# Down projections of a two-layer trunk: 24 instead of 18 of 44 weight pairs by seven products, 16 of them with weight block sums made in DRAM

## The chip, the cores and the metric

The kernel runs on one core of a Trainium2 chip. The metric is the device time in microseconds of one execution. Before the change it is 2559.3 us, the median of 3 runs (2558.61 to 2559.44).

## What is computed

One sequence of 256 tokens with a width of 2048 goes through two layers in float32: a retention layer and a block-sparse attention layer, each followed by a gated MLP with a causal convolution of three taps. D_FF is 5632. The part that is changed is the last product of each MLP:

```python
def conv_ffn(h, w_up, conv_w, conv_b, w_down):
    u = h @ w_up
    ch = u.shape[-1]
    u = lax.conv_general_dilated(
        u, conv_w.astype(u.dtype)[:, None, :], window_strides=(1,),
        padding=[(CONV_WIDTH - 1, 0)], dimension_numbers=('NWC', 'WIO', 'NWC'),
        feature_group_count=ch) + conv_b
    gate, val = jnp.split(u, 2, axis=-1)
    return (jax.nn.silu(gate) * val) @ w_down
...
    for i in range(DEPTH):
        ...
        h = h + conv_ffn(rms_norm(h, ffn_norm[i]), ffn_w_up[i], ffn_conv_w[i], ffn_conv_b[i], ffn_w_down[i])
    return rms_norm(h, final_norm)
```

`w_down` is 5632 x 2048 in each layer.

## The kernel before

**Precision.** Each float32 operand is split into a high part in fp32r and the remainder, and a product is three matmuls: high x high, high x low, low x high. The activations are split once and stay in SBUF (`actT`, `hT`, `yT`, `oT`). The weights stream in from DRAM, and each piece is split on the way: ACT writes `wh` (L226), DVE writes `wl` = `raw` - `wh` (L227), both in `split_to`.

**Units and halves.** A *unit* is 1 MB of weights, loaded by SP into one of four `raw` buffers (`issue_dma`, L168). It is split and used in *halves*: `step` issues the splits up to three halves ahead of the matmuls of the current half (`LOOKAHEAD`), and there are four buffers for `wh` and four for `wl`, one for each half in turn. A load waits until the unit four places back has been split. `later` holds functions that are run when a given half has been reached (`after`).

**Stages.** Eight retention heads, the retention's out projection, the up stage of layer 0 (44 panels of 4 halves, `panel_b`), its down projection, the attention, its out projection, the up stage of layer 1 and its down projection. A down projection is two panels (`panel_s`), one for each 1024 columns of `w_down`; a panel runs over 22 *pairs* of k blocks (2 x 128 rows).

**Eight and seven.** A pair is a product of 2 x 2 blocks: two k blocks of 128 rows, two blocks of 128 tokens, two blocks of 512 columns. Done plainly (`eight`) it is eight block products, 24 matmuls, in two halves of 12. Done by Strassen's method in Winograd's form (`seven`) it is seven, 21 matmuls, in four halves of 6, 3, 6 and 6. A seven needs sums of weight blocks and sums of activation blocks. DVE makes the weight sums in place in the `raw` buffer: L242 after the first half's split, L247 and L248 after the second's; the third and the fourth half's splits read them. The activation sums (*forms*) are made by DVE in the up stage, stored to DRAM (L1021), fetched by ACT's queue into one of eight slots in `hT` (L440) and split there by ACT and DVE (L445, L446) one pair before they are used.

**Order.** A string of letters gives each panel's order, A for a plain pair and S for a seven. Before, the first panel of a down projection has ten sevens, at the odd places from 3 to 21, and the second has eight, "AAASASASASASASASASAAAA". So in both panels each seven stands behind a plain pair. The order on each engine is then set by a scheduler that may move an instruction by a few places.

Of the kernel before, what the change touches and what calls it, by code (L numbers as in the profile page):

```python
# [17 lines left out]
P = 128  # L18
# [50 lines left out]
def wide_seqs(first, second, n_slots=8):  # L69


    n = len(second)
    one = [(p, first.index(p) % n_slots if p in first else None, p in first) for p in range(n)]
    again = [(i % n_slots, p, False) for i, p in enumerate(first)][-n_slots:]
    again += [(again[i][0], p, True) for i, p in enumerate(first[:-n_slots])]
    again = again[: second.count("S")]
    others = [p for p in range(n) if p not in [q for _, q, _ in again]]
    two = []
    for c in second:
        slot, p, fresh = again.pop(0) if c == "S" else (None, others.pop(0), False)  # L80
        two.append((p, slot, fresh))
    return one, two


def head_seq(pairs, seq, fresh):

    again, others = list(enumerate(pairs)), [p for p in range(len(seq)) if p not in pairs]
    return [(*again.pop(0)[::-1], fresh) if c == "S" else (others.pop(0), None, False) for c in seq]


FFN_SEVENS = list(range(3, 22, 2))
FFN_SEQS = wide_seqs(FFN_SEVENS, "AAASASASASASASASASAAAA")
RET_SEQS = wide_seqs([5, 7, 9, 11, 13, 15], "AAASASASASASAAAA")
HEAD_SEQS = [head_seq([0, 2, 4], "AASASASA", hd == 0) for hd in range(RH - 1)] + [head_seq([0, 2], "AASAASAA", False)]
MOB_V_SEQ = head_seq([0, 2, 4], "AASASASA", True)
MOB_SEQS = wide_seqs([3, 5, 7], "AAASAAAA")


def build(tc, a, out):
# [44 lines left out]
    halves = []  # L144
    state = {"dma": 0, "split": 0, "mm": 0}
# [93 lines left out]
    def split_b11_b22(raw, wh, wl):  # L239
        b = blocks(raw)  # L240
        split_to(blocks(wh), blocks(wl), b[:, 0:4:3, :])
        dve.tensor_tensor(b[:, 0:2, :], b[:, 0:4:3, :], b[:, 1:2, :].to_broadcast([P, 2, 512]), op=ALU.add)  # L242

# [121 lines left out]
    def panel_s(unit, xT, seq, temps, done, slots=hT_slot, end=None, before=None,  # L365
                stored=None):
# [42 lines left out]
        def fs(s, i):  # L409
            return [v[:, i * P : (i + 1) * P] for v in slots(s)]  # L410
# [39 lines left out]
        def seven(i, k, s):  # L450
# [151 lines left out]
    def out_proj(w, seqs, xT, temps, g0, use_r, stored=None):  # L602
# [9 lines left out]
        emit(panel_s(unit_s(w, 0), xT, seqs[0], temps, residual_s(0, temps), stored=stored))  # L612
        emit(panel_s(unit_s(w, 1024), xT, seqs[1], temps,
                     residual_s(2, temps, lambda: [transpose_first(i) for i in range(2)], rest), stored=stored))
# [242 lines left out]

    xT_h = [hT]
# [42 lines left out]
    for hd in range(RH):  # L901
        ret_head(hd)
# [86 lines left out]
    def ffn_layer(layer, begin, g_next, use_next, last):  # L989
# [5 lines left out]

        for j in range(NFB // 2):
# [28 lines left out]
        if not last:  # L1025
            return out_proj(wd, FFN_SEQS, actT, temps_ffn, g_next, use_next, stored)
# [7 lines left out]
        emit(panel_s(unit_s(wd, 0), actT, FFN_SEQS[0], temps_ffn, residual_s(0, temps_ffn), stored=stored))  # L1034
        emit(panel_s(unit_s(wd, 1024), actT, FFN_SEQS[1], temps_ffn, residual_s(2, temps_ffn, last=last_bank), end=4,
                     before=gains_first, stored=stored))
# [208 lines left out]
```

## Time and profile before

| | |
|---|---|
| median of 3 runs | 2559.3 us |
| the profiled execution | 2559.53 us |
| its span | 2557.4 us |
| DVE busy | 2107.6 us, 2766 instructions |
| ACT busy | 1447.6 us, 1870 instructions |
| POOL busy | 10.2 us, 24 instructions |
| moved by DMA | 504.41 MB, 197 GB/s on average |

The span runs from the first to the last instruction of the program. PE is TensorE's matmuls, PEld its weight loads (which run beside the matmuls), DVE VectorE, ACT ScalarE, POOL GpSimd, SP SyncE, which issues most loads. In lines of instructions, "L227 DVE TENSOR_TENSOR wl<-raw,wh" is an instruction of line 227 on DVE that writes the tile wl from raw and wh; "x3" merges three of them that follow one another; "[0.41 <-ACT wh L226]" says that the engine had been idle for 0.41 us and what ended that. Matmuls are pipelined: each takes longer than the distance to the next, so their starts are what to compare.

### The profile page before, as it was taken

The numbers are of one execution on the slowest core, as the hardware profiler recorded it, in microseconds if no ns is written. First come the engines' busy times: TensorE is split into PE (matmuls) and PEld (weight loads), VectorE is DVE, ScalarE is ACT, GpSimd is POOL, SyncE is SP. The second block draws the span as 40 slices with busy tenths as digits, with TensorE's granted clock in tenths as the row PEclk, the third lists the DMA queues.
The fourth block names the chain that finished last, engine by engine and source line by source line (L and its number), as shares of the span: only waits on it lengthen the run. The fifth ranks groups of instructions, "written<-read, shape, count | busy, mean of one in ns | idle before, by whom it ended". The sixth has DMA issues, their size and how long they took to land.

```text
span 2557.4 us, 34487 instructions
## 1 busy us (share of the span) xinstructions
PE 2545.5 (100%) x13277; PEld 2177.8 (85%) x13277; DVE 2107.6 (82%) x2766; ACT 1447.6 (57%) x1870; POOL 10.2 (0%) x24
## 2 busy tenths in 40 slices
PE   9999999999999999999999999999999999999998
PEld 8888888888888888888888888888888888888887
DVE  7888888998877777777898887768877777778997
ACT  6555555555565555555565655555655555555654
POOL 0000000000000000000000000000000000000000
PEclk9999999999999999999999999999999999999999
DMA  7665655555565656566665565555565656567654
GB/s 258 227 201 186 197 186 186 189 181 196 199 197 183 205 188 203 190 202 193 235 208 193 198 216 179 174 183 172 193 196 194 198 191 200 193 199 243 214 198 148
DMA packets 342196, 504.41 MB, mean 197 GB/s; under 512 B 9600, under 2 KB 260496, under 8 KB 341776
## 3 DMA queue, kind: packets, MB, share of 16 engines
q1 hardware_dynamic: 330672, 483.53, 57.2%
q10 hardware_dynamic: 11360, 18.69, 2.2%
q8 instruction: 104, 1.70, 0.3%
q14 instruction: 60, 0.49, 0.1%
HBM read 494.82 MB, written 10.51 MB: 198 GB/s over the span
## 4 chain that ended last, share of the span: by engine, by line
PE 95%; DVE 3%; ACT 1%; issue 1%; DMA 1%; SPq 0%; POOL 0%; POOLq 0%; ACTq 0%; DVEq 0%
PE acc L349 34%; PE aux L395 31%; PE acc L352 17%; PE acc L395 8%; DVE wl L227 1%; PE acc L315 1%; PE acc L317 1%; PE acc L316 1%; PE aux L529 0%; PE aux L528 0%; PE aux L527 0%; PE aux L545 0%; DMA raw<-in_ret_w_in_dram 0%; ACT wh L226 0%; PE acc L545 0%
## 5 line engine op out<-in xcount | busy, mean ns | idle before, releaser
L226 ACT ACTIVATE wh<-raw 128x1024 fp32r<-128x1024 f32 (+2 forms) x1067 | 1084.2, 1027 | 1005.4 <-PE acc L349 434.6
L227 DVE TENSOR_TENSOR wl<-raw,wh 128x1024 fp32r<-128x1024 f32 (+2 forms) x1067 | 1242.8, 1182 | 388.9 <-ACT wh L226 381.1
L349 PE MATMUL acc<-hT,wh 128*128 128x512 f32 x3840 | 1197.7, 393 | 1.0 <-DVE hT L551 0.8
L352 PEld LDWEIGHTS acc<-hT,wl 128*128 128x128 f32 x3840 | 720.4, 188 | 161.4 <-DVE wl L227 0.6
L352 PE MATMUL acc<-hT,wl 128*128 128x256 f32 x3840 | 761.3, 279 | 0.2 <-DVE wl L227 0.2
L349 PEld LDWEIGHTS acc<-hT,wh 128*128 128x128 f32 x3840 | 586.3, 188 | 3.0 <-ACT wh L226 1.6
L395 PE MATMUL aux<-wh,actT 128*128 128x512 f32 x976 | 319.3, 390 | 0.0
L395 PE MATMUL aux<-wh,hT 128*128 128x512 f32 x942 | 314.6, 390 | 0.4 <-ACT wh L226 0.2
L395 PEld LDWEIGHTS aux<-wh,actT 128*128 128x128 f32 x976 | 183.2, 188 | 38.6 <-DVE h L625 0.5
L395 PEld LDWEIGHTS aux<-wh,hT 128*128 128x128 f32 x942 | 176.7, 188 | 38.9 <-ACT wh L226 1.8
L395 PE MATMUL aux<-wl,actT 128*128 128x512 f32 x488 | 189.9, 389 | 0.0
L395 PE MATMUL aux<-wl,hT 128*128 128x512 f32 x471 | 183.8, 390 | 0.4 <-DVE wl L227 0.4
L934 DVE SCALAR_TENSOR_TENSOR t<-u,cw,t 128x256 f32<-128x256 f32 x352 | 146.7, 479 | 0.0
L395 PE MATMUL aux<-wh,yT 128*128 128x512 f32 x426 | 141.8, 391 | 0.4 <-ACT yT L226 0.4
L395 PE MATMUL acc<-wh,hT 128*128 128x512 f32 x358 | 131.6, 391 | 0.0
L395 PEld LDWEIGHTS aux<-wl,actT 128*128 128x128 f32 x488 | 91.6, 188 | 18.6
L395 PEld LDWEIGHTS aux<-wl,hT 128*128 128x128 f32 x471 | 88.4, 188 | 19.1 <-DVE wl L227 1.1
L395 PEld LDWEIGHTS aux<-wh,yT 128*128 128x128 f32 x426 | 80.0, 188 | 17.7 <-ACT yT L226 0.9
L930 ACT ACTIVATE t<-u,cw 128x256 f32<-128x256 f32 x176 | 94.9, 587 | 0.1
L242 DVE TENSOR_TENSOR raw<-raw 128x1024 f32<-128x1024 f32 x77 | 93.9, 1219 | 0.0
L395 PE MATMUL aux<-wl,yT 128*128 128x512 f32 x213 | 83.0, 390 | 0.0
L750 DVE TENSOR_TENSOR bs<-acc,bs 128x512 f32<-128x512 f32 x120 | 82.1, 684 | 0.0
(228 smaller groups left out, 1943.4 us busy)
## 6 DMA issues: line engine op xcount, KB each, us to landing
raw<-in_ffn_w_up_dram SPq DMA_DIRECT2D x176, 1024.0 KB, 5.1
raw<-in_ffn_w_down_dram SPq DMA_DIRECT2D x88, 1024.0 KB, 5.5
raw<-in_ret_w_in_dram SPq DMA_DIRECT2D x133, 512.0 KB, 4.7
raw<-in_moba_w_qkv_dram SPq DMA_DIRECT2D x48, 1024.0 KB, 5.3
raw<-in_ret_w_out_dram SPq DMA_DIRECT2D x32, 1024.0 KB, 5.5
raw<-in_ret_w_in_dram SPq DMA_DIRECT2D x29, 1024.0 KB, 5.7
raw<-in_moba_w_out_dram SPq DMA_DIRECT2D x16, 1024.0 KB, 5.4
f<-t ACTq DMA_DIRECT2D x20, 256.0 KB, 4.2
```

What stands on the lines that cost most here:

```text
L226: in_turn(act.activation(hi, src, AF.Copy))
L227: in_turn(dve.tensor_tensor(lo, src, hi.bitcast(F32), op=ALU.subtract))
L242: dve.tensor_tensor(b[:, 0:2, :], b[:, 0:4:3, :], b[:, 1:2, :].to_broadcast([P, 2, 512]), op=ALU.add)
L315: pe.matmul(acc, lhsT=xh, rhs=wh[:, c, :], start=(k == 0), stop=False)
L316: pe.matmul(acc, lhsT=xh, rhs=wl[:, c, :], start=False, stop=False)
L317: pe.matmul(acc, lhsT=xl, rhs=wh[:, c, :], start=False, stop=(k == nk - 1))
L349: pe.matmul(acc[:, b, :], lhsT=wh[:, c, b * P : (b + 1) * P], rhs=xt[:, k, :], start=(k == 0), stop=False)
L352: pe.matmul(acc[:, b, S:], lhsT=wl[:, c, b * P : (b + 1) * P], rhs=xt[:, k, :S], start=False, stop=(k == KC - 1))
L395: pe.matmul(acc[b], lhsT=xs, rhs=ws, start=(n == 1), stop=(n == uses[b]))
L750: dve.tensor_tensor(bs, acc[:, :, :S], bs, op=ALU.add)
L930: act.activation(t[:, i, :], u[:, i, 2:], AF.Identity, bias=c[:, 3, b : b + 1], scale=c[:, 2, b : b + 1])
L934: dve.scalar_tensor_tensor(t[:, i, :], u[:, i, tap : tap + S], c[:, tap, b : b + 1], t[:, i, :], op0=ALU.mult, op1=ALU.add)
```

## The change

In both layers 24 of the 44 pairs of a down projection are done by seven, 12 in each panel. Letters are A, S and now P: for a P the weight sums are not made by DVE. Long before, in the heads, the out projections, the attention and the up stages, a chain of transfers makes them in DRAM (`block_sums`): ACT's queue copies blocks of `w_down` into a DRAM tile of 4 x 128 x 512 (two copies of 512 KB), and POOL's queue adds to it with accumulating transfers of 256 KB each, two from `w_down`, then one from block to block, then another. The four steps of a chain are three halves apart (`place_chains`). There are 16 chains a layer.

A P is loaded as two units: three plain blocks (0.75 MB, by two loads), and the four sums from DRAM (1 MB). The first unit has the halves of 6 and 3 matmuls, the second those of 6 and 6. The new letters are "AAAPAPSAPAPSAPAPSAPAPS" and "AAAPSPAPSPAPSPAPSPAAAA". The forms of 12 pairs are stored instead of 10, and the second panel now fetches four of them again. The out projections' letters and the heads' stay what they were, written in another way.

```diff
+    sevens = [p for p in range(n) if first[p] != "A"]
+    one = [(p, sevens.index(p) % n_slots if p in sevens else None, p in sevens) for p in range(n)]
+    again = [(i % n_slots, p, False) for i, p in enumerate(sevens)][-n_slots:]
+    again += [(again[i][0], p, True) for i, p in enumerate(sevens[:-n_slots])]
+    again = again[: n - second.count("A")]
...
+def made_ahead(seq, letters):
+    return [p for (p, _, _), c in zip(seq, letters) if c == "P"]
...
-FFN_SEVENS = list(range(3, 22, 2))
-FFN_SEQS = wide_seqs(FFN_SEVENS, "AAASASASASASASASASAAAA")
+FFN_LETTERS = ("AAAPAPSAPAPSAPAPSAPAPS", "AAAPSPAPSPAPSPAPSPAAAA")
+FFN_SEQS = wide_seqs(*FFN_LETTERS)
+FFN_SEVENS = [p for p, slot, _ in FFN_SEQS[0] if slot is not None]
...
+        src = src() if callable(src) else src
         raws[u] = wraw.tile([P, 2048], F32, name="raw")
         dst = raws[u].rearrange("p (c n) -> p c n", n=n)
-        if len(src.shape) == 4:
+        if isinstance(src, list):
+            for c, v in src:
+                nc.sync.dma_start(dst[:, c : c + v.shape[1]], v)
+        elif len(src.shape) == 4:
...
+    def split_front(raw, wh, wl):
+        split_to(wh[:, :512], wl[:, :512], raw[:, 1024:1536])
...
             def u4_u2(wh, wl):
-                mul(4, xs(1, k + 1), wh[:, 0, :], wl[:, 0, :])
-                mul(6, fs(s, 2), wh[:, 1, :], wl[:, 1, :])
+                a, b = (0, 1) if made is None else (1, 0)
+                mul(4, xs(1, k + 1), wh[:, a, :], wl[:, a, :])
+                mul(6, fs(s, 2), wh[:, b, :], wl[:, b, :])
                 ends()
...
         for i, (pair, slot, _) in enumerate(seq):
             k = 2 * pair
-            mms = [(j, eight(i, j, k)) for j in range(2)] if slot is None else seven(i, k, slot)
-            items.append((unit(k), [(part, counted(mm)) for part, mm in mms]))
+            made = None if slot is None or sums is None else sums(pair)
+            mms = [(j, eight(i, j, k)) for j in range(2)] if slot is None else seven(i, k, slot, made)
+            mms = [(part, counted(mm)) for part, mm in mms]
+            if made is None:
+                items.append((unit(k), mms))
+                continue
+            items.append((made[0], [(0, mms[0][1]), (split_front, mms[1][1])]))
+            items.append((made[1], [(hf, mms[2 + hf][1]) for hf in range(2)]))
...
+    def block_sums(name, w, n0, pairs, apart=512):
+        summed = {}
+        n = w.shape[1]
+        def blk(pair, c, b, step=0, count=1):
+            off = w.offset + (2 * pair + c) * P * n + n0 + b * apart
+            return bass.AP(tensor=w.tensor, offset=off, ap=[[n, P], [step, count], [1, 512]])
+        def add(dst, src):
+            tc.keep_in_program_order(nc.gpsimd.dma_start(dst, src, accum_op=ALU.add, max_dma_last_dim=8192))
+        def copies(pair):
+            s = summed[pair] = dram.tile([4, P, 512], F32, name="wsum")
+            for i in (0, 2):
+                c, step = ((0, P * n + apart), (0, P * n))[i // 2]
+                tc.keep_in_program_order(dma0(s[i : i + 2].rearrange("b p n -> p b n"), blk(pair, c, 0, step, 2)))
+        def first(pair):
+            for i in range(2):
+                add(summed[pair][i], blk(pair, 0, 1)[:, 0, :])
+        def second(pair):
+            add(summed[pair][2], summed[pair][1])
+        def third(pair):
+            add(summed[pair][3], summed[pair][2])
+        def units_of(pair):
+            if pair not in pairs:
+                return None
+            plain = [(0, blk(pair, 0, 0, P * n + apart, 2)),
+                     (2, blk(pair, 1, 0))]
+            return (plain, 512), (lambda: summed[pair].rearrange("b p n -> p b n"), 512)
+        chains[name] = [[lambda f=f, p=p: f(p) for f in (copies, first, second, third)] for p in pairs]
+        return units_of
+    def place_chains(name, places):
+        while places and chains[name]:
+            at = places.pop(0)
+            for i, f in enumerate(chains[name].pop(0)):
+                later.append([at + 3 * i, f])
...
+        sums_of = [block_sums(("down", layer, i), wd, 1024 * i, made_ahead(FFN_SEQS[i], FFN_LETTERS[i])) for i in range(2)]
...
+    def places(*runs):
+        return [marks[name] + first + apart * i for name, first, apart, n in runs for i in range(n)]
+    early = places(*((("head", hd), 5, 0, 1) for hd in range(2, RH)), ("ret_out", 6, 30, 2), ("up0", 8, 20, 8))
+    late = places(("moba", 8, 18, 5), ("moba_out", 6, 0, 1), ("up1", 8, 16, 10))
+    for layer, p in enumerate((early, late)):
+        for i in range(2):
+            place_chains(("down", layer, i), p)
```

The change moves instructions on several engines. In the rows that follow, a name's number tells one tile from another; the line numbers behind the change are higher (L227 is L244, L242 is L259, L247 and L248 are L267 and L268, L446 is L466, L395 is L415).

DVE in the first down panel of layer 0, before: the last split of a plain pair (raw_11125), then a seven (raw_11144).

```order
L227 TENSOR_TENSOR wl_11213<-raw_11125,wh_11212 128x1024
L227 TENSOR_TENSOR wl_11225<-raw_11144,wh_11224 128x1024
L227 TENSOR_TENSOR wl_11236<-raw_11144,wh_11235 128x512
L242 TENSOR_TENSOR raw_11144<-raw_11144 128x1024
L247 TENSOR_TENSOR raw_11144<-raw_11144 128x512
L248 TENSOR_TENSOR raw_11144<-raw_11144 128x512
L446 TENSOR_TENSOR hT_116<-hT_116 128x512
L227 TENSOR_TENSOR wl_11256<-raw_11144,wh_11255 128x1024
L227 TENSOR_TENSOR wl_11272<-raw_11144,wh_11271 128x1024
```

The same with the change: the last split of a P (raw_11215, its unit of sums), then an S (raw_11234).

```order
L244 TENSOR_TENSOR wl_11284<-raw_11215,wh_11283 128x1024
L466 TENSOR_TENSOR hT_116<-hT_116 128x512
L244 TENSOR_TENSOR wl_11299<-raw_11234,wh_11298 128x1024
L244 TENSOR_TENSOR wl_11307<-raw_11234,wh_11306 128x512
L259 TENSOR_TENSOR raw_11234<-raw_11234 128x1024
L267 TENSOR_TENSOR raw_11234<-raw_11234 128x512
L268 TENSOR_TENSOR raw_11234<-raw_11234 128x512
L244 TENSOR_TENSOR wl_11319<-raw_11234,wh_11318 128x1024
L244 TENSOR_TENSOR wl_11329<-raw_11234,wh_11328 128x1024
```

The operations are the same; the split of the form has moved ahead of the seven's first split, and what stands ahead of the seven is now a half of a P. At the first three S of the second panel no such split lies between these rows; at the last S of the first panel a residual add (L652) lies between L267 and L268.

PE at the second and third half of the same seven, before:

```order
L395 MATMUL aux_10759<-wh_11235,actT_6346 128x512
L395 MATMUL acc_10882<-wh_11255,hT_116 128x512
L395 MATMUL acc_10882<-wl_11256,hT_116 128x512
L395 MATMUL acc_10882<-wh_11255,hT_116 128x512 x2
L395 MATMUL acc_10882<-wl_11256,hT_116 128x512
L395 MATMUL acc_10882<-wh_11255,hT_116 128x512
L395 MATMUL aux_10762<-wh_11271,actT_6346 128x512
```

And with the change:

```order
L415 MATMUL aux_10882<-wh_11306,actT_6402 128x512
L415 MATMUL acc_11005<-wh_11318,hT_116 128x512
L415 MATMUL aux_10885<-wh_11328,actT_6402 128x512
L415 MATMUL acc_11005<-wl_11319,hT_116 128x512
L415 MATMUL acc_11005<-wh_11318,hT_116 128x512 x2
L415 MATMUL acc_11005<-wl_11319,hT_116 128x512
L415 MATMUL acc_11005<-wh_11318,hT_116 128x512
L415 MATMUL aux_10885<-wl_11329,actT_6402 128x512
```

The first matmul of the fourth half (wh_11328) has moved ahead of the third half's first use of a wl (wl_11319).

SP in the first down panel with the change: two loads and the load of the sums for a P, one load for an S and for a plain pair; before, every row there was a load of 128x2x1024.

```order
L174 DMA raw_11186<-in_ffn_w_down_dram 128x2x512
L174 DMA raw_11186<-in_ffn_w_down_dram 128x512
L185 DMA raw_11215<-wsum_3390 128x4x512
L185 DMA raw_11234<-in_ffn_w_down_dram 128x2x1024
L185 DMA raw_11265<-in_ffn_w_down_dram 128x2x1024
```

Where SP had one load of a pair, it now has three for a P.

More of the change, by code (lines that the diff above doesn't have):

```diff
@@ L72, in wide_seqs @@
     n = len(second)
[L73 to L76, printed above, removed]
+    sevens = [p for p in range(n) if first[p] != "A"]
[3 more added lines that the diff above has]
+    again = again[: n - second.count("A")]
     others = [p for p in range(n) if p not in [q for _, q, _ in again]]
@@ L79, in wide_seqs @@
     for c in second:
-        slot, p, fresh = again.pop(0) if c == "S" else (None, others.pop(0), False)
+        slot, p, fresh = again.pop(0) if c != "A" else (None, others.pop(0), False)
         two.append((p, slot, fresh))
     return one, two
+def made_ahead(seq, letters):
+    return [p for (p, _, _), c in zip(seq, letters) if c == "P"]
 def head_seq(pairs, seq, fresh):
     again, others = list(enumerate(pairs)), [p for p in range(len(seq)) if p not in pairs]
-    return [(*again.pop(0)[::-1], fresh) if c == "S" else (others.pop(0), None, False) for c in seq]
-FFN_SEVENS = list(range(3, 22, 2))
-FFN_SEQS = wide_seqs(FFN_SEVENS, "AAASASASASASASASASAAAA")
[L93 to L96, printed above, removed]
+    out = []
+    for c in seq:
+        slot, p = again.pop(0) if c != "A" else (None, others.pop(0))
+        out.append((p, slot, slot in fresh))
+    return out
+FFN_LETTERS = ("AAAPAPSAPAPSAPAPSAPAPS", "AAAPSPAPSPAPSPAPSPAAAA")
+FFN_SEQS = wide_seqs(*FFN_LETTERS)
+FFN_SEVENS = [p for p, slot, _ in FFN_SEQS[0] if slot is not None]
+RET_SEQS = wide_seqs("AAAAASASASASASAS", "AAASASASASASAAAA")
+HEAD_LETTERS = ["AASASASA"] * (RH - 1) + ["AASAASAA"]
+HEAD_SEQS = [head_seq([0, 2, 4][: l.count("S")], l, range(3) if hd == 0 else ()) for hd, l in enumerate(HEAD_LETTERS)]
+MOB_V_SEQ = head_seq([0, 2, 4], "AASASASA", range(3))
+MOB_SEQS = wide_seqs("AAASASAS", "AAASAAAA")
 def build(tc, a, out):
@@ L144, in build @@
     halves = []
+    marks, chains = {}, {}
     state = {"dma": 0, "split": 0, "mm": 0}
@@ L365, in panel_s @@
     def panel_s(unit, xT, seq, temps, done, slots=hT_slot, end=None, before=None,
-                stored=None):
+                stored=None, sums=None):
         acc, count, uses, items, late = {}, {}, {}, [], []
@@ L448, in opens, with seven @@
                 make_forms(seq[i + 2][1], 2 * seq[i + 2][0])
-        def seven(i, k, s):
+        def seven(i, k, s, made):
             def b11_b22(wh, wl):
@@ L600, in make_rB, with out_proj @@
         use(pt[:, 0, :])
-    def out_proj(w, seqs, xT, temps, g0, use_r, stored=None):
+    def out_proj(w, seqs, xT, temps, g0, use_r, stored=None, sums=(None, None)):
         def transpose_first(i):
@@ L610, in rest @@
             after(3, lambda: use_r())
-        emit(panel_s(unit_s(w, 0), xT, seqs[0], temps, residual_s(0, temps), stored=stored))
+        emit(panel_s(unit_s(w, 0), xT, seqs[0], temps, residual_s(0, temps), stored=stored, sums=sums[0]))
         emit(panel_s(unit_s(w, 1024), xT, seqs[1], temps,
-                     residual_s(2, temps, lambda: [transpose_first(i) for i in range(2)], rest), stored=stored))
+                     residual_s(2, temps, lambda: [transpose_first(i) for i in range(2)], rest), stored=stored, sums=sums[1]))
     def residual_s(j, temps, sevens_done=None, all_done=None, last=None):
@@ L856, in ret_yT @@
         to_T(yT[0], 4 * hd, lambda t, c: y[:, t, c * P : (c + 1) * P], 64 + 4 * hd, 4)
+    def block_sums(name, w, n0, pairs, apart=512):
[31 more added lines that the diff above has]
+                later.append([at + 3 * i, f])
+        assert not chains[name]
     xT_h = [hT]
@@ L901, in build @@
     for hd in range(RH):
+        marks["head", hd] = len(halves)
         ret_head(hd)
@@ L1025, in ffn_layer @@
         if not last:
-            return out_proj(wd, FFN_SEQS, actT, temps_ffn, g_next, use_next, stored)
+            return out_proj(wd, FFN_SEQS, actT, temps_ffn, g_next, use_next, stored, sums_of)
         def gains_first():
@@ L1032, in gains_first @@
                     after(6 + 2 * j + t, lambda j=j, t=t: gain_final(j, t))
-        emit(panel_s(unit_s(wd, 0), actT, FFN_SEQS[0], temps_ffn, residual_s(0, temps_ffn), stored=stored))
+        emit(panel_s(unit_s(wd, 0), actT, FFN_SEQS[0], temps_ffn, residual_s(0, temps_ffn), stored=stored, sums=sums_of[0]))
         emit(panel_s(unit_s(wd, 1024), actT, FFN_SEQS[1], temps_ffn, residual_s(2, temps_ffn, last=last_bank), end=4,
-                     before=gains_first, stored=stored))
+                     before=gains_first, stored=stored, sums=sums_of[1]))
     def ffn_begin(prev):
@@ L1209, in moba, with mark @@
                 emit(panel_a(w_qkv, KC, 2 * D + g * 512, xT_h, v_done))
+    def mark(name):
+        marks[name] = len(halves)
+    mark("ret_out")
     out_proj(a["ret_w_out"][0], RET_SEQS, yT, make_temps(lambda: ret["p1"], af="bs", ff="m1", m="qT"), 32, lambda: make_rB(use_rB))
+    mark("up0")
     ffn_layer(0, ffn_begin("ret"), 16, lambda: make_rB(use_mob), False)
+    mark("moba")
     moba()
+    mark("moba_out")
     out_proj(a["moba_w_out"][0], MOB_SEQS, oT, make_temps(lambda: mob["p2"], af="qT0", ff="qT1", m="kT0"), 48, lambda: make_rB(use_rB))
+    mark("up1")
     ffn_layer(1, ffn_begin("mob"), None, None, True)
+    def places(*runs):
[5 more added lines that the diff above has]
+            place_chains(("down", layer, i), p)
     run()
```

## The prediction

> **What bounds the kernel now.** I read the profile's first part, then its chain, then stretches of the two kinds of panel, then one period of the first down panel instruction by instruction.
>
> ```profile
> PE 2545.5 (100%) x13277; PEld 2177.8 (85%) x13277; DVE 2107.6 (82%) x2766; ACT 1447.6 (57%) x1870; POOL 10.2 (0%) x24
> ...
> PE 95%; DVE 3%; ACT 1%; issue 1%; DMA 1%; SPq 0%; POOL 0%; POOLq 0%; ACTq 0%; DVEq 0%
> ```
>
> PE is busy for all but 12 us of 2557.4, and the chain that ended last runs through PE for 95%. So a matmul removed is worth its time, and any microsecond for which PE is made to wait is lost in full.
>
> ```profile
> core 0: us, PE busy (x) PEld busy (x) DVE busy (x) ACT busy (x) POOL busy (x), PEclk, DMA share, GB/s
> 740.00:1220.00 480.00, 480.00 (x2771) 421.75 (x2770) 368.41 (x503) 272.08 (x346) 0.00 (x0) 1.00 0.60 196
> 1221.00:1335.00 114.00, 114.00 (x505) 94.37 (x504) 105.85 (x117) 70.42 (x80) 0.00 (x0) 1.00 0.61 211
> ```
>
> The first row is the up stage of layer 0, the second its first down panel. In the down panel DVE is busy 105.85 of 114 us, with PE still at 114. On average the change relieves DVE; the question is whether DVE is on time at each place.
>
> One period of that panel follows: the last matmul of a seven (1302.99), a plain pair (from 1303.21), the next seven (from 1308.65).
>
> ```profile
> 1302.30 2.96 DVE L227 TENSOR_TENSOR wl<-raw,wh 128x1024 fp32r<-128x1024 f32 x3
> ...
> 1302.99 0.39 PE L395 MATMUL acc<-wh,hT 128*128 128x512 f32 x1
> 1303.21 0.39 PE L395 MATMUL aux<-wh,actT 128*128 128x512 f32 x1
> ...
> 1305.17 1.22 DVE L242 TENSOR_TENSOR raw<-raw 128x1024 f32<-128x1024 f32 x1
> 1306.43 0.69 DVE L247 TENSOR_TENSOR raw<-raw 128x512 f32<-128x512 f32 x1
> 1307.15 0.69 DVE L248 TENSOR_TENSOR raw<-raw 128x512 f32<-128x512 f32 x1
> 1307.76 0.69 DVE L446 TENSOR_TENSOR hT<-hT 128x512 fp32r<-128x512 f32 x1
> 1308.37 1.22 DVE L227 TENSOR_TENSOR wl<-raw,wh 128x1024 fp32r<-128x1024 f32 x1
> ...
> 1308.65 0.39 PE L395 MATMUL acc<-wh,actT 128*128 128x512 f32 x1
> ...
> 1308.90 1.06 ACT L226 ACTIVATE wh<-raw 128x1024 fp32r<-128x1024 f32 x1 [1.33 <-PE aux L395]
> 1310.00 1.23 DVE L227 TENSOR_TENSOR wl<-raw,wh 128x1024 fp32r<-128x1024 f32 x1 [0.41 <-ACT wh L226]
> ...
> 1310.69 0.39 PE L395 MATMUL acc<-wh,hT 128*128 128x512 f32 x1
> 1310.92 0.39 PE L395 MATMUL acc<-wl,hT 128*128 128x512 f32 x1
> ```
>
> Three things come out of it.
>
> First, the price of a matmul: the plain pair, 24 matmuls, runs from 1303.21 to 1308.65, 5.44 us, so 0.227 us each. A seven, 21 matmuls, takes 4.76 us: its halves take 1.36, 0.68, 1.36 and 1.36. A plain half takes 2.72.
>
> Second, how far the split runs ahead. There are four wh and four wl buffers, one for each half, so a half's split waits until PE has finished the half four places earlier. At 1308.65 PE has left the plain pair's last half; ACT starts the split that waited for it at 1308.90, and DVE its part at 1310.00. So **DVE starts 1.35 us after PE frees the buffer**.
>
> Third, the run that DVE has to do for a seven. At 1302.30 it starts the last split before the seven; then come both splits of the seven's first two halves, the block sums L242, L247 and L248, the split of a stored form (L446), and from 1308.37 to 1309.59 the wl of the seven's third half. That is **7.28 us without a gap**. PE wants that wl at 1310.92, so today 1.33 us are to spare.
>
> **The change, part by part.** *Removed:* 12 pairs (6 a layer) lose one product of three matmuls: 36 x 0.227 = **8.2 us** off PE. This term is sure, as PE is always busy there.
>
> *The new wait.* A seven made ahead (P) puts no sums on DVE, but it lasts 4.76 us where a plain pair lasts 5.44, and above all in halves of 1.36, 0.68, 1.36 and 1.36. In the new letters each of the 4 sevens a panel whose sums DVE still makes (S) stands right behind a P, never behind a plain pair. The four halves that PE works off while DVE prepares an S were 1.36 + 1.36 + 2.72 + 2.72; they get shorter.
>
> Let T be the time when PE starts the P. The last split before S is P's last half; its buffer is the one PE frees at T. DVE starts it at T + 1.35. The same list of operations as above then ends at T + 1.35 + 7.28 = T + 8.63. PE reaches the wl of S's third half after P (4.76), S's first two halves (2.04) and one matmul (0.23), at T + 7.03. **PE waits 1.60 us.**
>
> Where no form is to be split, the list is 0.60 shorter (1307.76 to 1308.37), but then the split of S's first half waits for the buffer that P's first half frees at T + 1.36, and starts on DVE at T + 2.71; from there 7.28 - 0.60 - 1.13 = 5.55 us (1.13: the spacing of two wl in the run of three, from 2.27 us for two) lead to T + 8.26, and PE waits 1.23 us. The new PE order lets the fourth half's wh matmul go ahead of the third's wl; it wants the wh behind L248, which ACT ends at about T + 8.6 too, so that gains nothing.
>
> By the new DVE order a form's split lies in the run at the four S of the first panel and at the last S of the second, not at the other three. At the last S of the first panel one residual add (0.6 us) lies in it as well. A layer: 5 x 1.60 + 3 x 1.23 + 0.6 = 12.3 us; two layers **24.6 us**. Behind the late wl on DVE's queue stand only the next splits; they have recovered by the next plain pair, whose halves are long, and the P that follows an S gets its first wl 0.2 us or more early. So I count nothing more there.
>
> *Weight loads in the down panels.* A P loads 0.75 + 1 MB where a pair loaded 1 MB.
>
> ```profile
> raw<-in_ffn_w_down_dram SPq DMA_DIRECT2D x88, 1024.0 KB, 5.5
> raw<-in_ret_w_in_dram SPq DMA_DIRECT2D x133, 512.0 KB, 4.7
> ...
> f<-t ACTq DMA_DIRECT2D x20, 256.0 KB, 4.2
> hT<-f ACTq DMA_DIRECT2D x20, 256.0 KB, 5.5
> skewD<-tblD ACTq DMA_DIRECT2D x1, 3072.0 KB, 12.5
> ```
>
> A load starts when the unit four places back is split, so at least three units' matmuls lie between its start and its need: the shortest three, 2.72 + 4.76 + 2.04, give 9.5 us against 5.5 to land. In bytes: A P A P S loads 6.5 MB (6.82e6 bytes) and three forms (0.79e6) in 25.2 us, 302 GB/s.
>
> ```profile
> 1215.00:1220.00 5.00, 5.00 (x31) 4.37 (x30) 3.18 (x6) 2.76 (x3) 0.00 (x0) 1.00 0.99 326
> ```
>
> At a share of 0.99 the engines moved 326 GB/s, with two queues at work. So 302 fits, at 93%. I take nothing; if the mix only reached 290, the two first panels (111 us each) would lose 4%, 9 us. More than one queue with 2 KB rows never ran that long before, so a loss is open, a gain excluded.
>
> *The chains in DRAM.* For each P: two copies (1.05e6 bytes) issued by ACT, four accumulating transfers of 256 KB by POOL. No row shows an accumulate. The nearest is skewD, DRAM to DRAM: 3.15e6 bytes in 12.5 us, 252 GB/s. [...]
>
> ```profile
> 1214.67 0.62 PE L349 MATMUL acc<-hT,wh 128*128 128x512 f32 x2
> ...
> 1217.44 0.62 PE L349 MATMUL acc<-hT,wh 128*128 128x512 f32 x2
> ```
>
> [...] Cost: nothing. [...]
>
> *On the queues.*
>
> ```profile
> 1242.22 0.33 ACTq L440 DMA_DIRECT2D hT<-f  x1
> ...
> DVE sg L852 <- POOL rs L583: 1.6, 8, 0.2
> ```
>
> 64 copies and 16 more stores and fetches on ACT cost 0.33 us each to issue; ACT is idle for 43%. On POOL the accumulates wait for one another, each three halves on; the only other work behind them is the eight pow of the heads, six others and the memsets at the up stages' starts, and none follows a chain sooner than some ten halves. SP issues two loads more for a P, without work of its own. DVE forms of two more pairs in each up stage, about 1.2 us each, lie in the 111 us that DVE is idle there. All nothing; each is hidden by the time named.
>
> **The sum**, against the profiled execution (2559.5 us with the span of 2557.4; the median of the runs is 2559.3, the same): 2559.5 - 8.2 + 24.6 = **2576 us**.
>
> **Rivals.**
> 1. *The S is in time behind a P*, and only the removed matmuls count: 2559.5 - 8.2 = 2551. For it: DVE loses 20 sets of sums, 52 us. It decides at a run of 5.68 us (7.03 - 1.35) in place of 7.28. Against it: every operation of the run is in the new order, one behind the other, and their spacings are those of the period above. Half of the wait would give 2564.
> 2. *The DMA engines are the limit*, on top of the waits. [...] With only the loads of the down panels short (290 GB/s), 2585. For it: a share of 0.99 was reached once already. [...]
> 3. *The sums aren't ready when they are loaded*, so SP waits. The last chain begins 24 halves (66 us) before the end of the up stage, and its pair is one of the second panel, over 110 us on. It doesn't happen.
>
> **How the numbers follow.** The forecast with its bounds (2564 to 2585) 0.74; rival 1 0.11; rival 2 0.14; rival 3 0.01. Of the forecast, 0.05 lies where half of the wait or less comes true, within 0.2% (5.1 us, about what a measurement of this kernel tells from no change). So faster 0.11, same 0.05, slower 0.84. The range reaches from 2564 (half the wait) into the milder part of rival 2, 2590.
>
> **What would show it.** In the after profile: 36 matmuls fewer; 16 waits of PE for a DVE wl or an ACT wh in the third half of each S, 1.2 to 1.6 us (2.2 at two), and no others; DMA share under 0.9 in both up stages; landing times of the loads up by some us without a wait. I am wrong if PE's wait at an S behind a P is under 0.5 us, or if PE waits in the up stage.

## The result, and the profile after

| | before | after |
|---|---|---|
| median | 2558.8 us (6 runs, 2558.4 to 2559.4) | 2581.3 us (6 runs, 2581.0 to 2581.5) |
| the profiled execution, its span | 2559.5, 2557.4 us | 2581.5, 2579.7 us |
| matmuls | 13277 | 13241 |

The kernel became slower: the ratio is 1.0087, with a 95% interval of 1.0074 to 1.010. 36 matmuls are gone, and 22.5 us were added.

The first part of the changed kernel's page (busy time, share of the span, instructions) and its chain of waits, as shares of the span:

```profile
PE 2547.9 (99%) x13241; PEld 2170.3 (84%) x13241; DVE 2091.8 (81%) x2754; ACT 1467.2 (57%) x1906; POOL 114.2 (4%) x152
...
PE 90%; DVE 6%; ACT 2%; issue 1%; DMA 1%; POOL 0%; ACTq 0%; POOLq 0%; DVEq 0%
```

DVE has less to do than before (2091.8 us, not 2107.6) and yet its share of the chain went from 3% to 6%. PE was idle for 12 us of the span and is now for 32. The view of who waited for whom on PE (total, times, longest, in us) names the place; the first two rows are of the changed kernel, the third is all that the kernel before had of them:

```profile
PE aux L415 <- ACT wh L243: 16.9, 19, 1.4
PE acc L415 <- ACT wh L243: 2.9, 11, 0.3
...
PE aux L395 <- ACT wh L226: 0.2, 1, 0.2
```

One of the 16 places, each an S behind a P, is the counterpart of the period shown in the prediction. From the timeline of the changed kernel (start, duration, instruction, idle time before it and what ended that):

```profile
1303.01 0.39 PE L415 MATMUL acc<-wh,actT 128*128 128x512 f32 x1
...
1304.30 1.23 DVE L244 TENSOR_TENSOR wl<-raw,wh 128x1024 fp32r<-128x1024 f32 x1 [1.49 <-ACT wh L243]
...
1305.44 0.68 DVE L466 TENSOR_TENSOR hT<-hT 128x512 fp32r<-128x512 f32 x1
...
1306.05 1.82 DVE L244 TENSOR_TENSOR wl<-raw,wh 128x1024 fp32r<-128x1024 f32 x2
...
1307.78 1.22 DVE L259 TENSOR_TENSOR raw<-raw 128x1024 f32<-128x1024 f32 x1
...
1309.12 1.06 ACT L243 ACTIVATE wh<-raw 128x1024 fp32r<-128x1024 f32 x1 [2.86 <-DVE raw L259]
...
1309.58 0.39 PE L415 MATMUL aux<-wh,actT 128*128 128x512 f32 x1
1309.76 0.69 DVE L268 TENSOR_TENSOR raw<-raw 128x512 f32<-128x512 f32 x1
...
1310.23 0.49 PE L415 MATMUL acc<-wh,hT 128*128 128x512 f32 x1 [0.26 <-ACT wh L243]
1310.37 3.65 DVE L244 TENSOR_TENSOR wl<-raw,wh 128x1024 fp32r<-128x1024 f32 x3
1310.57 2.96 ACT L243 ACTIVATE wh<-raw 128x1024 fp32r<-128x1024 f32 x3 [0.39 <-DVE raw L268]
...
1311.68 0.50 PE L415 MATMUL aux<-wh,actT 128*128 128x512 f32 x1 [0.95 <-ACT wh L243]
...
1312.01 0.40 PE L415 MATMUL acc<-wl,hT 128*128 128x512 f32 x1
```

PE starts the P at T = 1303.01. DVE begins the P's last split at T + 1.29; from there it works without a gap until the wl of the S's third half, which starts at 1310.37. PE ends the S's second half with the matmul of 1309.58, waits for the third half's wh (which ACT could make only when L259 was done), does one matmul at 1310.23, and then waits for the fourth half's wh, which hangs on L268. By the starts of its matmuls, which stand 0.227 us apart elsewhere, PE loses 0.42 us behind the matmul of 1309.58, 1.22 us behind that of 1310.23 and 0.11 us behind that of 1311.68 (here and below this last part is called the restart): 1.75 us. Over the 16 places, 27.1 us: ten with a form's split (L466) in the run, at 1.73 to 2.23, and six without, at 1.33 to 1.47 but for one of 1.78. At that one and at the one of 1.47, in the second panels, the period began late: ACT had waited 2.4 us for a P's sums to land (to 2489.1 and 1379.2), and PE loses 0.45 and 0.14 us more than at their like.

The rest of the difference is in two places that the prediction does not have.

DVE in the retention's output stage, at the border of its two panels, in the changed kernel:

```profile
636.68 1.22 DVE L259 TENSOR_TENSOR raw<-raw 128x1024 f32<-128x1024 f32 x1
640.15 0.69 DVE L652 TENSOR_TENSOR h<-aux,h 128x512 f32<-128x512 f32 x1 [2.25 <-PE aux L415]
640.76 0.69 DVE L267 TENSOR_TENSOR raw<-raw 128x512 f32<-128x512 f32 x1
641.36 1.22 DVE L244 TENSOR_TENSOR wl<-raw,wh 128x1024 fp32r<-128x1024 f32 x1
642.49 0.69 DVE L268 TENSOR_TENSOR raw<-raw 128x512 f32<-128x512 f32 x1
```

A residual add (L652) that wants a finished bank of PE now stands between two block sums of a seven. DVE stands still for 2.25 us until PE has got there, L267 and L268 come late, and PE loses 1.6 us between 642 and 646. Before, the add (there L625) stood behind all the block sums and the split:

```profile
636.54 1.22 DVE L242 TENSOR_TENSOR raw<-raw 128x1024 f32<-128x1024 f32 x1
637.79 0.69 DVE L247 TENSOR_TENSOR raw<-raw 128x512 f32<-128x512 f32 x1
638.52 0.69 DVE L248 TENSOR_TENSOR raw<-raw 128x512 f32<-128x512 f32 x1
639.13 1.22 DVE L227 TENSOR_TENSOR wl<-raw,wh 128x1024 fp32r<-128x1024 f32 x1
640.27 0.68 DVE L625 TENSOR_TENSOR h<-aux,h 128x512 f32<-128x512 f32 x1
```

And the granted clock behind one of the two longest of the 16 waits, in three stretches of the changed kernel (busy us and instructions of each engine, granted clock, DMA share, GB/s):

```profile
1337.20:1340.20 3.00, 1.57 (x6) 1.09 (x7) 3.00 (x5) 2.22 (x3) 0.00 (x0) 1.00 0.08 33
1340.30:1343.70 3.40, 3.40 (x9) 2.67 (x9) 3.40 (x4) 1.69 (x2) 0.00 (x0) 0.50 0.53 131
1343.80:1347.00 3.20, 3.20 (x16) 2.61 (x15) 3.20 (x6) 2.15 (x4) 0.00 (x0) 1.00 0.90 299
```

For 3.4 us TensorE's granted clock was 0.50: 9 matmuls where the next stretch, a little shorter, has 16. That costs 1.7 us, and PE counts as busy in it, so it appears in no view of waits.

The sum for the profiled execution: 2559.5 - 8.2 (matmuls) + 27.1 (S behind a P) + 1.6 (output stage) + 1.7 (half clock) = 2581.7, against 2581.5.

The DMA engines are busier, and in the up stages PE never waits for them. The two up stages after the change, in the same columns:

```profile
742.00:1221.00 479.00, 479.00 (x2766) 420.91 (x2765) 369.35 (x509) 271.64 (x346) 25.83 (x32) 1.00 0.77 232
1856.00:2325.00 469.00, 469.00 (x2708) 412.22 (x2707) 361.13 (x496) 266.57 (x339) 32.27 (x40) 1.00 0.82 240
```

The DMA share rises from 0.60 to 0.77 and 0.82; PE is busy for the whole of both. The loads land later there, 6.5 us after their issue in the median (x176, 1024 KB each), where they took 5.1 before (the first row is after, the second before):

```profile
raw<-in_ffn_w_up_dram SPq DMA_DIRECT2D x176, 1024.0 KB, 6.5
...
raw<-in_ffn_w_up_dram SPq DMA_DIRECT2D x176, 1024.0 KB, 5.1
```

### The profile page after: what moved, and what is told of

It reads as the page before. It is cut to its first block, busy times and chain, and to the rows that moved or that the text cites. A ratio compares the mean times of both kernels' runs of the same rounds, so it can differ in the third digit from the quotient of the medians.

```text
span 2579.7 us, 34946 instructions
## 1 busy us (share of the span) xinstructions
PE 2547.9 (99%) x13241; PEld 2170.3 (84%) x13241; DVE 2091.8 (81%) x2754; ACT 1467.2 (57%) x1906; POOL 114.2 (4%) x152
## 4 chain that ended last, share of the span: by engine, by line
PE 90%; DVE 6%; ACT 2%; issue 1%; DMA 1%; POOL 0%; ACTq 0%; POOLq 0%; DVEq 0%
PE acc L369 34%; PE aux L415 28%; PE acc L372 17%; PE acc L415 7%; DVE wl L244 2%; ACT wh L243 2%; DVE raw L259 1%; DMA raw<-in_ffn_w_down_dram 1%; PE acc L335 1%; PE acc L337 1%; PE acc L336 1%; DVE raw L267 1%; DVE raw L268 1%; PE aux L572 0%; PE aux L556 0%
## 5 line engine op out<-in xcount | busy, mean ns | idle before, releaser
L243 ACT ACTIVATE wh<-raw 128x1024 fp32r<-128x1024 f32 (+2 forms) x1091 | 1099.0, 1022 | 974.0 <-PE acc L369 407.6
L244 DVE TENSOR_TENSOR wl<-raw,wh 128x1024 fp32r<-128x1024 f32 (+2 forms) x1091 | 1263.5, 1177 | 397.3 <-ACT wh L243 386.6
L415 PE MATMUL aux<-wh,hT 128*128 128x512 f32 x966 | 323.9, 390 | 0.4 <-ACT wh L243 0.2
L415 PE MATMUL aux<-wh,actT 128*128 128x512 f32 x832 | 279.6, 392 | 16.2 <-ACT wh L243 16.2
L415 PEld LDWEIGHTS aux<-wh,hT 128*128 128x128 f32 x966 | 181.2, 188 | 39.7 <-ACT wh L243 1.8
L415 PEld LDWEIGHTS aux<-wh,actT 128*128 128x128 f32 x832 | 156.7, 188 | 53.1 <-ACT wh L243 21.1
L415 PE MATMUL aux<-wl,hT 128*128 128x512 f32 x483 | 188.5, 390 | 0.4 <-DVE wl L244 0.4
L415 PE MATMUL acc<-wh,hT 128*128 128x512 f32 x430 | 159.9, 397 | 2.9 <-ACT wh L243 2.9
L415 PE MATMUL aux<-wl,actT 128*128 128x512 f32 x416 | 162.1, 390 | 0.0
L415 PE MATMUL aux<-wh,yT 128*128 128x512 f32 x426 | 142.3, 391 | 1.0 <-ACT wh L243 0.6
L415 PEld LDWEIGHTS aux<-wl,hT 128*128 128x128 f32 x483 | 90.7, 188 | 19.7 <-DVE wl L244 1.1
L415 PEld LDWEIGHTS acc<-wh,hT 128*128 128x128 f32 x430 | 81.0, 188 | 25.4 <-ACT wh L243 9.1
L896 POOL DMA_DIRECT2D wsum<-in_ffn_w_down_dram x64 | 53.8, 841 | 1047.9 <-DMA wsum<-in_ffn_w_down_dram 864.4
L415 PEld LDWEIGHTS aux<-wh,yT 128*128 128x128 f32 x426 | 79.9, 188 | 19.0 <-ACT wh L243 1.4
L415 PEld LDWEIGHTS aux<-wl,actT 128*128 128x128 f32 x416 | 78.2, 188 | 16.2
```

The costliest lines, as they stand in the source:

```text
L243: in_turn(act.activation(hi, src, AF.Copy))
L244: in_turn(dve.tensor_tensor(lo, src, hi.bitcast(F32), op=ALU.subtract))
L415: pe.matmul(acc[b], lhsT=xs, rhs=ws, start=(n == 1), stop=(n == uses[b]))
L896: tc.keep_in_program_order(nc.gpsimd.dma_start(dst, src, accum_op=ALU.add, max_dma_last_dim=8192))
```

## The experiments

Times are medians, ratios are to the kernel before with 95% intervals. Every experiment is an edit to the changed kernel, unless it says otherwise.

**Every S behind a plain pair.** Same 12 sevens a panel, 8 P and 4 S.

```diff
-FFN_LETTERS = ("AAAPAPSAPAPSAPAPSAPAPS", "AAAPSPAPSPAPSPAPSPAAAA")
+FFN_LETTERS = ("AAPAPASPAPASPAPASPAPAS", "AAASPPASPPASPPASPPAAAA")
```

> Theory W (PE waits in the third half of each S that stands behind a P): with the same 12 sevens a panel, 8 P and 4 S, but every S behind a plain pair, the 16 waits go (together with the slow restart of PE they add up to 26.8 us in the trace of the change), and with them the 3.4 us at half the clock behind one of them (1.7 us): 2581.3 - 28.5 = 2553 us, 0.25% under the kernel before. Theory D (the DMA engines are short, by the chains or by the larger loads of a P): bytes and chains are the same, so the time stays within some 3 us of 2581, and the waits of PE move to other places.

2559.8 us (2558.2 to 2561.9), ratio 1.0004 [0.9995, 1.0013]. The 16 waits are gone, and 21.5 of the 28.5 us that were expected to go with them; 2553 us was not reached. The first panels (P A P A S) have no wait left. In the second ones new waits stand, some 6 us in the profiled run, mostly where two P meet (A S P P). Two loads of the second panel of layer 0, with the split that waited and the matmul that waited for it (timeline; then, for the first load alone, the time from issue to landing; then two stretches in the columns used above):

```profile
1376.12 2.64 SPq L185 DMA_DIRECT2D raw<-in_ffn_w_down_dram  x2
...
1384.48 2.00 ACT L243 ACTIVATE wh<-raw 128x1024 fp32r<-128x1024 f32 x2 [2.55 <-DMA raw<-in_ffn_w_down_dram]
...
1386.85 0.50 PE L415 MATMUL aux<-wl,actT 128*128 128x512 f32 x1 [0.76 <-DVE wl L244]
```

```profile
DMA to landing us min/median/max: 8.3/8.3/8.3
```

```profile
1374.00:1378.00 4.00, 4.00 (x19) 3.29 (x18) 4.00 (x5) 3.35 (x5) 0.00 (x0) 1.00 0.50 163
1378.00:1385.00 7.00, 7.00 (x32) 5.80 (x32) 4.55 (x5) 3.45 (x5) 0.00 (x0) 1.00 1.00 356
```

The plain pair's weights behind two P were issued at 1376.12 and landed 8.3 us later, in a stretch where all DMA engines are busy; ACT starts their split at 1384.48, and DVE's part of it ends too late for PE. So theory W holds for the S, and theory D is right about something smaller than it claimed: two P side by side ask for 3.5 MB within four buffers, and the next load comes late.

**No chains, plain blocks in place of the sums.**

```diff
-            return (plain, 512), (lambda: summed[pair].rearrange("b p n -> p b n"), 512)
+            again = [(0, blk(pair, 0, 0, apart, 2)), (2, blk(pair, 1, 0, apart, 2))]
+            return (plain, 512), (again, 512)
...
-            place_chains(("down", layer, i), p)
+            pass
```

> No copies and accumulates in DRAM at all; the second unit of a P loads 1 MB of the plain weight blocks in place of the sums, so the product of the sums is left out of what is right. Theory W: the 16 waits of PE stay as they are; only the 1.6 us in the retention's output stage go, if they come from the order that a chain there brings with it: 2579.7 us. Theory D: with 134 MB less moved by the DMA engines the waits shrink, 2551 to 2565 us.

2579.2 us (2577.2 to 2580.7), ratio 1.0078 [1.0066, 1.0091]. This kernel leaves out the sums, so its down projections are not the model's; its loads into `raw` are as large as before. All 16 waits stand, 26.5 us in all against 27.1; the waits at 642 us are gone. (By the profile the chains move 67 MB, not the 134 of the expectation.) Sums made in DRAM have no part in the loss at the S.

**The chain of the output stage elsewhere.**

```diff
-    early = places(*((("head", hd), 5, 0, 1) for hd in range(2, RH)), ("ret_out", 6, 30, 2), ("up0", 8, 20, 8))
+    early = places(*((("head", hd), 5, 0, 1) for hd in range(2, RH)), ("ret_out", 14, 30, 2), ("up0", 8, 20, 8))
```

> The changed kernel with the first chain of the retention's output stage started at half 14 of it, not 6. Theory W with O (the place of the chain put a residual add ahead of two block sums on DVE's queue, where it waits for PE): the order there is again that of the kernel before, the three waits of PE near 642 us go, 2579.7 us, the 16 waits at S stay. If those three waits come from the transfers beside them, they stay or move with the chain: 2581.3 us.

2579.3 us (2577.2 to 2579.7), ratio 1.0076 [1.0062, 1.009]. DVE at the same border of the panels:

```profile
636.13 1.22 DVE L259 TENSOR_TENSOR raw<-raw 128x1024 f32<-128x1024 f32 x1
637.39 0.69 DVE L267 TENSOR_TENSOR raw<-raw 128x512 f32<-128x512 f32 x1
638.11 0.69 DVE L268 TENSOR_TENSOR raw<-raw 128x512 f32<-128x512 f32 x1
638.72 1.22 DVE L244 TENSOR_TENSOR wl<-raw,wh 128x1024 fp32r<-128x1024 f32 x1
639.86 0.69 DVE L652 TENSOR_TENSOR h<-aux,h 128x512 f32<-128x512 f32 x1
```

This run is called ret_place below. The residual add is behind the sums again, and PE waits for nothing there. That the chain's place, and not its traffic, does it follows from the order: instructions of a chain, which stand on ACT's and POOL's queues, were enough for the scheduler to place an add on DVE differently. Which of them did it was not tried. In this kernel's trace PE loses 1.0 us at 2348.7, at the start of layer 1's down projection, where the changed kernel loses nothing and the kernel before 0.45; ACT stands there for 4.8 us until a form has gone to DRAM. Its five runs lie in two groups, 2577.2 and 2579.3 to 2579.7; the profiled one, of 2579.7, has a granted clock of 0.50 from 2448.3 to 2451.6 us, behind the longest wait of layer 1, and none in layer 0.

**Chains alone.** The letters of the kernel before; the sums are made and not loaded; the output stage's chain at 14.

```diff
-FFN_LETTERS = ("AAAPAPSAPAPSAPAPSAPAPS", "AAAPSPAPSPAPSPAPSPAAAA")
+FFN_LETTERS = ("AAASASASASASASASASASAS", "AAASASASASASASASASAAAA")
...
-            if pair not in pairs:
-                return None
+            return None
...
-        sums_of = [block_sums(("down", layer, i), wd, 1024 * i, made_ahead(FFN_SEQS[i], FFN_LETTERS[i])) for i in range(2)]
+        sums_of = [block_sums(("down", layer, i), wd, 1024 * i, [3, 5, 8, 10, 13, 15, 18, 20]) for i in range(2)]
```

> The letters of the kernel before (18 sevens, all S), with all 32 chains in DRAM issued and their sums never loaded; the chain of the retention's output stage starts at half 14, not 6. Theory W: the chains cost nothing, 2559 us, within 2 us. Theory D, chains: PE waits in up stages or panels for loads that land late, over 2564 us.

2558.8 us (2558.4 to 2559.1), ratio 1.0 [0.9991, 1.0009]. The chains are free. Their DMA queues (packets, MB, share of 16 engines' span):

```profile
q0 software_dynamic: 12288, 33.56, 8.2%
q10 hardware_dynamic: 28768, 52.25, 7.3%
```

q0 holds the accumulates: 8.2% of the span of 2557.3 us is 210 us, 6.55 us of all engines a chain, 1.64 us an accumulate. q10 had 18.69 MB and 2.2% before; the 5.1% more are the copies, 4.08 us a chain. So a chain takes 10.6 us. The same 1.05e6 bytes took 6.55 us as accumulates against 4.08 as copies, a rate of 0.62.

**Sevens in pairs, without any P.** An edit to the kernel before: its 18 sevens at other places.

```diff
-FFN_SEVENS = list(range(3, 22, 2))
-FFN_SEQS = wide_seqs(FFN_SEVENS, "AAASASASASASASASASAAAA")
+FFN_SEVENS = [4, 5, 8, 9, 12, 13, 16, 17, 20, 21]
+FFN_SEQS = wide_seqs(FFN_SEVENS, "AAASSAASSAASSAASSAAAAA")
```

> The kernel before, without any P, chain or new seven: only the places of its 18 sevens are changed, so that every second one stands right behind another seven (A A S S). Theory W (a seven in front of an S shortens the four halves for which DVE works ahead, whoever made its sums): nine S a layer stand behind a seven, five of them with a form's split in DVE's run (1.75 us each, with the restart, as in the trace of the change) and four without (1.33 us): 2 x 14.1 = 28 us, 2558.8 + 28 = 2587 us, and 1.7 us more for each stretch at half the clock that a wait brings. Theory P (the wait is a property of the P: its loads, its sums in DRAM, its split in two units): no waits, 2559 us.

2591.0 us (2589.9 to 2593.4), ratio 1.0127 [1.0113, 1.0141]. The second S of a pair, DVE and then PE (timeline):

```profile
1267.39 0.68 DVE L446 TENSOR_TENSOR hT<-hT 128x512 fp32r<-128x512 f32 x1
...
1271.71 0.69 DVE L248 TENSOR_TENSOR raw<-raw 128x512 f32<-128x512 f32 x1
1272.32 3.65 DVE L227 TENSOR_TENSOR wl<-raw,wh 128x1024 fp32r<-128x1024 f32 x3
...
1272.17 0.50 PE L395 MATMUL acc<-wh,hT 128*128 128x512 f32 x1 [0.31 <-ACT wh L226]
1273.62 0.50 PE L395 MATMUL aux<-wh,actT 128*128 128x512 f32 x1 [0.95 <-ACT wh L226]
```

The same two waits, with the same releasers, at 18 places: 1.8 us with a form's split, 1.42 without, and three of 2.3 to 2.4, 31.4 us in all, where 28 had been expected; behind one of them stands a stretch of 3.4 us at a granted clock of 0.50. This is the clearest of the runs: with no P, no chain and no larger load, a seven that stands behind a seven costs what the change's S behind a P costs.

**P in place of S, apart.** 18 sevens a layer, no S behind a P; the output stage's chain at 14.

```diff
-FFN_LETTERS = ("AAAPAPSAPAPSAPAPSAPAPS", "AAAPSPAPSPAPSPAPSPAAAA")
+FFN_LETTERS = ("AAASAPAPAPAPAPAPAPAPAS", "AAAPAPAPAPAPAPAPAPAAAA")
```

> The 18 sevens of the kernel before at nearly its places, 16 of them P in place of S and each behind a plain pair, so no S stands behind a P; the chain of the output stage starts at half 14. As many matmuls as before. Theory W: no waits of PE in the panels, 2559 us; DVE loses 16 sets of sums a layer and gains nothing for the time. Theory D, loads: 1.75 + 1 MB in 10.2 us (283 GB/s, and the forms) cost PE waits for weights that land late, 2562 us or more.

2559.0 us (2558.6 to 2560.7), ratio 1.0001 [0.9992, 1.001]. A P that stands alone costs nothing, its loads included. Taking 32 sets of block sums off DVE gains nothing either.

**A form's split earlier.** ret_place, with:

```diff
-                if i + 1 < len(seq) and seq[i + 1][2]:
-                    hi, lo = slots(seq[i + 1][1])
+                if i + 2 < len(seq) and seq[i + 2][2]:
+                    hi, lo = slots(seq[i + 2][1])
```

> ret_place (the changed kernel, its letters kept, the chain at half 14) with a form's split made two pairs ahead of its seven, not one, so that it lies ahead of the run of operations that DVE does for an S behind a P, no longer in it. Theory W: the five waits a layer with a form's split in the run (0.42 + 1.22 + 0.11 us) become like those without (1.22 + 0.11), 10 x 0.42 = 4.2 us less than ret_place: 2573.0 without a stretch at half the clock, 2575 with one. If DVE's run doesn't set the wait, nothing changes: 2577.2 or 2579.3.

2574.4 us (2573.8 to 2575.2), ratio 1.0061 [1.0047, 1.0075]. In the first panels all four places fall to 1.31 to 1.38 us, the last one from 2.2; in the second panels one place more than before has a form in its run. The 16 places add up to 23.3 us, against 26.7 in ret_place: 3.4 us less, not the 4.2 expected, mostly for that one place. So the wait follows the length of DVE's run: with the form's split out of it, the 0.42 us are gone.

**Only the last S of the first panel behind a plain pair.** ret_place, with:

```diff
-FFN_LETTERS = ("AAAPAPSAPAPSAPAPSAPAPS", "AAAPSPAPSPAPSPAPSPAAAA")
+FFN_LETTERS = ("AAPAPSAPAPSAPAPSAPAPAS", "AAAPSPAPSPAPSPAPSPAAAA")
```

> ret_place with one plain pair of the first panel moved from its start to the place ahead of its last S, so that this S alone stands behind a plain pair; the three S before it keep their places behind a P, as do the four of the second panel. Theory W: the longest wait of each layer goes, 2 x 2.2 = 4.4 us, and the others stay: 2572.8 us. Theory C (a stretch of 3.4 us at half the clock follows a loss of 2.2 us or more at one S, and none of 1.8 us or less): no such stretch is left, so the runs no longer lie in groups 2 us apart (ret_place: 2577.2 and 2579.3 to 2579.7), all within 1 us of 2572.8. If half-clock stretches don't depend on that wait, the two groups stay, 2573 and 2575.

2573.2 us (2573.1 to 2573.4, one run 2574.3), ratio 1.0057 [1.0043, 1.007]. The two waits of 2.2 us go, 14 of 1.33 to 2.03 stay, and the two groups of runs are gone. That all runs would lie within 1 us of 2572.8 held but for the one at 2574.3, the profiled one; its trace has no stretch at half the clock in the panels, and one place, at 2490.9, that lost 0.7 us more than its like.

**Versions that beat both.** 24 sevens a layer, two P together only once a layer; then 26 in the order S P A; then the same with one more plain pair at the second panel's end. All with the output stage's chain at 14.

```diff
+FFN_LETTERS = ("AAPAPASPAPASPAPASPAPAS", "AAPPASPAPASPAPASPASPAA")   (first)
+FFN_LETTERS = ("AASPASPASPASPASPASPASP", "AAASPASPASPASPASPASPAA")   (second)
+FFN_LETTERS = ("AASPASPASPASPASPASPASP", "AASPASPASPASPASPASPAAA")   (third)
```

> 24 sevens a layer, 16 P and 8 S, every S behind a plain pair, and two P next to each other only once a layer, at the start of the second panel (in s_behind_plain that was so four times a layer, and PE waited there for loads); the chain of the output stage starts at half 14. Theory W: 36 matmuls off, no waits at the S: 2558.8 - 8.2 = 2550.6 us, and up to 1.5 us a layer where the two P meet: 2550.6 to 2553.6. If P loads also come late where a P stands alone, 2556 or more.

> 26 sevens a layer, 13 P and 13 S, in the order S P A: every S behind a plain pair, every P behind an S, never P behind P. 48 matmuls fewer than the kernel before (8 pairs a layer of 3 matmuls each, 10.9 us). Theory W: the halves ahead of an S are those of the kernel before (a seven, then a plain pair), so DVE is in time: 2558.8 - 10.9 = 2548 us. If P's loads behind an S come late, or DVE falls behind over two sevens in a row, PE waits at each of the 26 P or S: 2 x 13 x 0.5 us or more, over 2560.

> spa with the second panel's sevens one pair earlier, so that three plain pairs and not two stand at its end (two at its start, not three). If the waits of PE around 1445 us (1.4 us for a transposed row, 0.3 behind it) come from sevens that stand too near to the panel's end, they go: 2551.7 - 1.7 = 2550 us. If the S that now stands third in the panel meets DVE's residual adds, PE waits 1 us or more there in each layer instead: 2552 or more.

First: 2553.6 us (2553.2 to 2554.0), ratio 0.998 [0.9971, 0.9989]. Second: 2551.7 us (2551.2 to 2552.6), ratio 0.9972 [0.9962, 0.9983]. Third: 2552.3 us (2552.0 to 2553.6), ratio 0.9975 [0.9965, 0.9985]. In none does an S lose the 1.3 us or more of the changed kernel, and in the first no S loses anything. What is left in the second's view of PE's waits:

```profile
PE aux L415 <- ACT hT L575: 1.4, 1, 1.4
PE acc L369 <- DVE hT L578: 1.2, 2, 0.8
```

The first row is the border between layer 0's down projection and the attention, where sevens now stand close to the panel's end. The third version, made to remove it, has in its place one wait of 1.4 us for another step of the same border (the diagonal of L625), and 0.6 us in each layer at the S that now stands third in the second panel, where residual adds lie between its block sums: the expectation of 2550 was wrong. The second version stays 3.7 us over its expectation. Its trace, by the starts of the matmuls, shows where: against the kernel before it loses 2.3 us more at the border, the first row's wait with its restart among them; 1.3 us at three S that begin before the split of their form (L466) is done (0.3, 0.3 and 0.7); and 1.2 us behind the last matmul, whose start is followed by 9.6 us of other work, in place of 8.5, where two plain pairs stand at the panel's end. With three there, in the third version, it is 8.6.

## Why the prediction was right, and by how much its terms were off

The direction and the mechanism held; the forecast was 2576 us, the measured 2581.3.

- *36 matmuls, 8.2 us.* Right in number (13277 to 13241), and shown to be worth their time as soon as no S stands behind a seven: 24 sevens come to 2553.6 us, 5.2 less than before, though not the whole 8.2: that version, too, loses some 2.3 us at the border behind the down projection of layer 0 and 1.2 behind the last matmul.
- *The wait at S behind a P: 1.60, 1.23, and 0.6 more at one.* Measured 1.75, 1.33 to 1.47, and 2.23. The run began at T + 1.29, where 1.35 had been taken. The form's split is worth 0.42 us and the residual add 0.47. What was left out is the restart of PE, 0.11 us a place. That makes 27.1 us, not 24.6. The prediction let PE wait once, for DVE's wl of the third half; in the trace PE waits for ACT's wh, of the third half where a form's split is in the run, and then at every place of the fourth half; they hang on L259 and L268. The size is the same, as the prediction had said of the fourth half's wh, because that wl and that wh are ready at nearly the same time. The cause as put there, that the halves ahead of the S are short, is shown by the pairs of S, where nothing else of the change is present.
- *"PE waits ... and no others."* This step failed. A wait of 1.6 us appeared in the retention's output stage, at an add whose place in DVE's order the prediction did not look at. It had counted the chains' issues at nothing because ACT and POOL have time; the run with the chain of the output stage elsewhere shows that the place of a chain's issues also decides what the scheduler puts where on another engine.
- *A wait costs its length.* Not quite: behind one of the two longest the granted clock was 0.50 for 3.4 us, which cost 1.7 us, and the sum had no term for it.
- *The chains.* Free, as predicted (chains alone: 2558.8). The prediction put their cost at nothing, an estimate: no row of the kernel before shows an accumulate. Measured with the chains alone, an accumulate takes 1.64 us of all engines and a chain 10.6. In the up stage of layer 1 the copies of one chain and the next are issued 44.4 us apart (1921.09, 1965.46, 2009.83): 10.6 of 44.4 is 0.24, and the DMA share rose there by 0.22, from 0.60 to 0.82, so there was room.
- *The loads of a P.* Free where a P stands alone (the run with P in place of S, apart), as predicted. The reason given, 9.5 us of lead against 5.5 to land, is too kind: where two P meet, a load took 8.3 us and its split, on ACT and then on DVE, some 2.4 more, and PE waited. In the letters of the change no two P meet, and late loads cost PE only 0.6 us there (the 0.45 and 0.14 above); so rival 2 did not come true. The 5.5 us to land did not hold even there: on the changed kernel's page the 1 MB loads from `w_down` land after 6.5 us in the median, those of the sums after 7.9. So the term came out near nothing because the lead had room, and not because the loads kept their time. The 290 GB/s of rival 2 are no ceiling: in the 7 us that end with that load the DMA engines moved 356 GB/s.
- *DMA share under 0.9 and later landings in the up stages, without a wait*: as foretold, 0.77 and 0.82, 6.5 us.

Open: which of a chain's issues moved the add in the output stage, and what decides whether a loss of 2.2 us is followed by a granted clock of 0.50.

## What to carry to other kernels

When one engine works a fixed number of pieces ahead, its lead is the time of the pieces that the consumer has in hand, so making pieces shorter takes lead from the next long preparation, even if the shortening itself costs that engine nothing: place short pieces so that a long one stands ahead of each preparation. A lower busy share of the helper engine says nothing about that; walk one period instruction by instruction. After adding even a few instructions to a queue, look at the whole order of every engine, not only at the stages that the edit is about.

## What was not expected of the hardware

TensorE's granted clock fell to 0.50 for 3.4 us, some 0.3 to 1.2 us after the longest wait there had ended, in the changed kernel, in the one with the chain of the output stage elsewhere and in the kernel with sevens in pairs. Each time it was behind the last S of a first panel, where PE loses 2.2 to 2.3 us within some 3 us. It followed 3 of the 9 places that lost 2.2 us or more in four traces (these three and the one without chains), and none of the places that lost 2.03 us or less. Taking away the loss of 2.2 us in both layers took away the groups of runs 2 us apart.

So the same loss can cost another 1.7 us or nothing. In the changed kernel's trace PE waits 0.26 and 1.43 us at the last S of layer 0's first panel (the matmuls of 1337.16 and 1339.09) and 0.27 and 1.43 us at that of layer 1 (2448.75 and 2450.67), a loss of 2.2 us each time by the starts; behind the first the granted clock was 0.50 from 1340.3 to 1343.7 us, behind the second it was 1.00 throughout (three stretches of 3 us from 2451 to 2460). What decides it, no run here shows.
